# Low-weight matmuls of a merged product moved behind the high-weight ones, in the FFN of a hybrid decoder layer

## The chip, the cores and the metric

The kernel runs on one core of one Trainium2 chip. The metric is the device time of one execution in microseconds (us); lower is better. A core has TensorE (PE, with its weight loads as PEld), VectorE (DVE), ScalarE (ACT), GpSimd (POOL) and SyncE (SP), which issues most of the transfers.

## The reference

One decoder layer over a sequence of 512 with a width of 2048, all in float32. Four mixers share an input projection and an output projection, then comes a gated MLP with a causal depthwise convolution, then a last norm:

```python
D_MODEL = 2048; SEQ = 512; FFN_DIM = 5504; MIX_W = 512
...
h = rmsnorm(x, norm_mix_g[l])
proj = h @ w_in[l]
s5_u, cv_v, cv_g, lru_x, lru_g, pool_x = jnp.split(proj, split_idx, axis=-1)
...
mixed = jnp.concatenate([y_s5, y_cv, y_lru, y_pool], axis=-1)
x = x + mixed @ w_out[l]
h = rmsnorm(x, norm_ffn_g[l])
x = x + conv_gated_mlp(h, ffn_w_up[l], ffn_w_dw[l], ffn_b_dw[l], ffn_w_down[l])
...
def conv_gated_mlp(h, w_up, w_dw, b_dw, w_down):
    up = h @ w_up
    gate, val = jnp.split(up, 2, axis=-1)
    gate = causal_dwconv(gate, w_dw, b_dw)
    return (jax.nn.gelu(gate, approximate=True) * val) @ w_down
```

## The kernel before

Tensors lie with the model's width on the 128 partitions and the 512 positions of the sequence in the free dimension. Every float32 operand of a matmul is split in two fp32r parts: ScalarE casts it to a high part (`split_to`, the CAST on L106), VectorE subtracts that from the original to get the low part (the TENSOR_TENSOR on L60). A normal product (`mm3`) is three matmuls of 512 columns: high weights by high data, high weights by low data, low weights by high data.

The FFN's up and down projections are mostly done by a scheme that replaces eight block products by seven products of sums and differences of blocks, called forms (a, b, d, r1, r2, r3, r4). In those the two halves of the data, 256 columns each, lie side by side in one tile as [high | low]. The high weights of a block take one matmul of 512 columns over both halves; the low weights take one of 256 columns over the high half alone, added to columns 256 to 511 of the same bank. This is the merged product that the change touches. It stands in two functions, both called `product`:

- in `ffn_up` (L1239 to L1249), 40 output tiles by 7 forms, 280 products, each of 8 blocks `p`. Data are the tiles X0 to X7, weights `uh<form>` and `ul<form>`.
- in `seven` (L1442 to L1452), called once for each of two groups of the down projection, 8 pairs of output tiles by 7 forms, so 56 products each, of 7 blocks. Data are the tiles Y (index Y5_0 to Y5_6 in the first group), weights `dh<form>` and `dl<form>`.

Weights come as tiles of 1024 (up) or 896 columns (down) on SP's queue; for r1 and r3 a second load on GpSimd's queue adds another block in place. They are staged two products ahead; the high and low tiles have three buffers each. In `ffn_up` the finished bank is copied out whole, by `after`; in `seven` two VectorE additions of 256 columns each (`xn<-xn,pa` and `xn<-xn,pb`) add the bank's halves to the residual, which lies in the tiles xn.

Before each `seven`, `eights` does five ordinary tiles of the down projection (L1352), eight output banks at a time; the first time ScalarE copies the banks to xn (L1375). Meanwhile `forms_dn` (L1386) loads pairs of stored activations as tiles `ap` (ap5_0 to ap5_6, two buffers) on SP's queue, and makes the Y tiles from them: casts on ScalarE, and sums, multiplications and subtractions on VectorE. Its last operation, a cast and a subtraction of 4 x 256 columns, completes the forms r4, r1, r3, d and r2.

TensorE's order in these stages is the program's order. A scheduler sets the order of the other engines and of SP's queue, from a cost model of its own.

Of the kernel before, what the change touches and what calls it, by code (L numbers as in the profile page):

```python
# [15 lines left out]
P = 128  # L16
# [28 lines left out]
NP2 = 7  # L45
# [4 lines left out]
class Kernel:  # L50
# [1144 lines left out]
    def ffn_up(self, xf, rp, rstd, ub):  # L1195
        tc, nc, a = self.tc, self.nc, self.a
        IX = {"a": 0, "b": 1, "r4": 2, "r1": 3, "r2": 4, "r3": 5, "d": 6}
# [41 lines left out]
        def product(k):  # L1239
            f, form = seq[k]  # L1240
            wh, wl = staged.pop(k)
            new = form in ("a", "b", "r1")
            if new:
                bank[f, form] = self.pa() if form == "b" else self.pb() if f % 2 else self.pa()
            ps = bank[f, {"a": "a", "r2": "a", "r3": "a", "d": "a", "b": "b", "r1": "r1", "r4": "r1"}[form]]
            for p in range(8):
                x, c = xf[p][:, IX[form]], slice(p * P, p * P + P)
                self.mm(ps, wh[:, c], x.rearrange("p n c->p (n c)"), new and p == 0, False, True)
                self.mm(ps[:, 256:512], wl[:, c], x[:, 0], False, p == 7, True)  # L1249

        two = lambda t: t.rearrange("p (n c)->p n c", n=2)
        quad = lambda tag, f: ub.tile([P, 2, 2, 256], F32, tag=tag, name=f"{tag}_{f}")
# [38 lines left out]
        for k in range(len(seq)):  # L1291
            with tc.high_priority(self.hp):
                load(k + LD)
                stage(k + AH)
            product(k)
            after(k)
# [108 lines left out]
    def seven(self, g):  # L1405
        tc, nc, a = self.tc, self.nc, self.a
        W = NP2 * P
        IX = {"a": 0, "b": 1, "r4": 2, "r1": 3, "r3": 4, "d": 5, "r2": 6}
        seq = [(0, x) for x in ("a", "r1", "r2", "b", "r3")]
        for j in range(1, 9):  # L1410
            for form, back in (("a", 0), ("d", 1), ("r1", 0), ("r4", 1), ("r2", 0), ("b", 0), ("r3", 0)):
                if j - back < 8:
                    seq.append((j - back, form))
        raws, staged, bank = {}, {}, {}
        blk = lambda j, x: a["w_dns"][g, j + 8 * (x in "cd"), :, int(x in "bd")]

        def load(k):
            if k >= len(seq):
                return
            j, form = seq[k]  # L1420
            if form in ("r2", "r4"):
                return
            t = (self.wp if form == "d" else self.rp).tile([P, 1024], F32, tag="raw", name=f"d{form}{g}_{j}")[:, 0:W]
            raws[j, form] = t
            nc.sync.dma_start(t, blk(j, "c" if form in ("r1", "r3") else form))
            if form in ("r1", "r3"):
                nc.gpsimd.dma_start(t, blk(j, "d" if form == "r1" else "a"), accum_op=ADD)

        def stage(k):
            if k >= len(seq):  # L1430
                return
            j, form = seq[k]
            if form in ("r2", "r4"):
                t = raws[j, "r1"]
                self.tt(t, t, raws[j, "a" if form == "r2" else "b"], ADD)
                raws[j, form] = t
            hi = self.wq.tile([P, 1024], F32R, tag="hi", name=f"dh{form}{g}_{j}")[:, 0:W]
            lo = self.wq.tile([P, 1024], F32R, tag="lo", name=f"dl{form}{g}_{j}")[:, 0:W]
            self.split_to(hi, lo, raws[j, form])
            staged[k] = (hi, lo)  # L1440

        def product(k):  # L1442
            j, form = seq[k]
            wh, wl = staged.pop(k)
            new = form in ("a", "b", "r1")
            if new:
                bank[j, form] = self.pa() if form == "b" else self.pb() if j % 2 else self.pa()
            ps = bank[j, {"r2": "a", "r3": "a", "d": "a", "r4": "r1"}.get(form, form)]
            for p in range(NP2):
                x, c = self.xf[p][:, IX[form]], slice(p * P, p * P + P)  # L1450
                self.mm(ps, wh[:, c], x.rearrange("p n c->p (n c)"), new and p == 0, False, True)
                self.mm(ps[:, 256:512], wl[:, c], x[:, 0], False, p == NP2 - 1, True)  # L1452
            up, half, op = {"a": (0, 0, ADD), "b": (0, 0, ADD), "r2": (0, 1, ADD), "r4": (0, 1, ADD),
                            "r3": (8, 1, SUB), "r1": (8, 1, SUB), "d": (8, 0, SUB)}[form]
            x = self.x2[j + up][:, 256 * half:256 * half + 256]
            for i in range(2):
                self.tt(x, x, ps[:, 256 * i:256 * i + 256], op)

        LD, AH = 6, 2
        for k in range(LD):  # L1460
            with tc.high_priority(self.hp):
                load(k)
        yield None
        for k in range(AH):
            with tc.high_priority(self.hp):
                stage(k)
            yield None
        for k in range(len(seq)):
            with tc.high_priority(self.hp):
                load(k + LD)  # L1470
                stage(k + AH)
            product(k)
            if g == 0 and seq[k][1] == "r3" and seq[k][0] < 6:
                self.resid2(seq[k][0] + 2)
                self.resid2(seq[k][0] + 10)
            yield len(seq) - 1 - k
# [139 lines left out]
```

## Time and profile before

| | |
|---|---|
| median of 3 runs | 1885.39 us (1875.49 to 1887.56) |
| the profiled execution's own time | 1886.01 us |
| its span, first to last instruction | 1884.0 us |
| TensorE busy | 1832.3 us, 97% of the span |
| VectorE busy | 1580.4 us, 84% |
| ScalarE busy | 905.9 us, 48% |

The profile is of one execution. In the timeline, times of matmuls begin when they start and overlap with the next one; ends are modelled. "xN" at a row's end counts instructions that were merged into one row, which starts with the first of them. Brackets name what ended the idle time before a row.

### The profile page before, as it was taken

The page shows a single profiled execution, that of the slowest core. Times are in us where ns is not written, and L with a number is a line of the kernel's source. Part 1 is how long each engine was busy: PE and PEld are TensorE (multiplying, and loading weights), DVE is VectorE, ACT ScalarE, POOL GpSimd, SP SyncE. Part 2 cuts the span into 40 slices and gives each one's busy share as a digit, 9 for nine tenths or more (in the row PEclk, how much of TensorE's full clock was granted, in tenths as well). Part 3 has the DMA queues.
Part 4 walks back from the last instruction along what each step waited for, and adds up shares of the span by engine and source line. Part 5 has one row for each costly group of instructions (what it writes and reads, how often), then busy time and mean ns, then how long its engine had stood idle before and what let it go on. Part 6 is the DMA issues. An engine that isn't in the chain of part 4 may idle for free.

```text
span 1884.0 us, 25963 instructions
## 1 busy us (share of the span) xinstructions
PE 1832.3 (97%) x9610; PEld 1548.0 (82%) x9610; DVE 1580.4 (84%) x2385; ACT 905.9 (48%) x1181; POOL 209.5 (11%) x291
## 2 busy tenths in 40 slices
PE   8999999999899999999999999999999999999996
PEld 6788887888788888888888888888888788788885
DVE  8699989998695788888888888888887889878965
ACT  6322446432573555555555555555555434433443
POOL 6210020202000000000000000000001210001000
PEclk9999999999999999999999999999999999999998
DMA  6232222523345777777777777777748975577623
GB/s 207 91 97 93 94 92 93 168 84 96 106 168 169 209 192 197 201 200 203 193 203 207 193 198 199 203 207 191 200 117 269 253 202 147 165 220 188 152 83 108
DMA packets 111870, 313.56 MB, mean 166 GB/s; under 512 B 15808, under 2 KB 21952, under 8 KB 111744
## 3 DMA queue, kind: packets, MB, share of 16 engines
q1 hardware_dynamic: 91920, 249.25, 39.4%
q0 software_dynamic: 19536, 62.14, 19.6%
q8 instruction: 75, 1.23, 0.3%
q10 hardware_dynamic: 288, 0.52, 0.1%
q14 instruction: 51, 0.42, 0.1%
HBM read 289.71 MB, written 19.66 MB: 164 GB/s over the span
## 4 chain that ended last, share of the span: by engine, by line
PE 85%; DVE 7%; DMA 4%; ACT 2%; issue 1%; POOL 0%; DVEq 0%; SPq 0%; ACTq 0%; POOLq 0%
PE pa L97 55%; PE pb L97 30%; DVE lo L60 1%; DMA ap<-act 1%; DMA raw<-w_dn 1%; DMA ur<-w_up 1%; DMA raw<-w_a 1%; ACT hi L106 1%; DVE X L60 1%; DVE M L60 0%; DVE o L60 0%; DVE bk L60 0%; DVE A L63 0%; DMA av<-act 0%; DVE l_x L63 0%
## 5 line engine op out<-in xcount | busy, mean ns | idle before, releaser
L97 PE MATMUL pa<-A,hi 128*128 128x512 f32 x1312 | 413.6, 397 | 15.0 <-ACT A L73 7.3
L97 PEld LDWEIGHTS pa<-A,hi 128*128 128x128 f32 x1312 | 246.9, 190 | 74.3 <-ACT A L73 7.7
L106 ACT CAST uhr<-ur 128x1024 fp32r<-128x1024 f32 x160 | 168.0, 1050 | 228.8 <-PE pb L97 120.2
L97 PE MATMUL pa<-A,lo 128*128 128x512 f32 x656 | 258.0, 396 | 2.3 <-DVE lo L60 2.2
L60 DVE TENSOR_TENSOR ulr<-ur,uhr 128x1024 fp32r<-128x1024 f32 x160 | 195.5, 1222 | 57.2 <-ACT uhr L106 57.2
L106 ACT CAST hi<-raw 128x1024 fp32r<-128x1024 f32 (+2 forms) x128 | 132.6, 1037 | 216.3 <-PE pa L97 166.5
L97 PE MATMUL pb<-X,uhr 128*128 128x512 f32 x640 | 231.3, 401 | 1.2 <-ACT uhr L106 1.2
L97 PE MATMUL pa<-X,uhr 128*128 128x512 f32 x640 | 229.7, 399 | 0.0
L60 DVE TENSOR_TENSOR lo<-raw,hi 128x1024 fp32r<-128x1024 f32 (+2 forms) x128 | 158.4, 1239 | 47.9 <-ACT hi L106 47.4
L97 PE MATMUL pb<-X,ulr 128*128 128x256 f32 x640 | 180.6, 282 | 0.8 <-DVE ulr L60 0.8
L97 PE MATMUL pa<-X,ulr 128*128 128x256 f32 x640 | 179.7, 281 | 0.0
L1222 POOL DMA_DIRECT2D ur<-w_up x80 | 70.0, 875 | 816.3 <-DMA ur<-w_up 564.9
L97 PEld LDWEIGHTS pa<-A,lo 128*128 128x128 f32 x656 | 124.3, 190 | 31.4 <-DVE lo L60 3.1
L97 PEld LDWEIGHTS pb<-X,uhr 128*128 128x128 f32 x640 | 121.0, 189 | 31.7 <-ACT uhr L106 1.5
L97 PEld LDWEIGHTS pa<-X,uhr 128*128 128x128 f32 x640 | 120.3, 188 | 30.0
L97 PEld LDWEIGHTS pb<-X,ulr 128*128 128x128 f32 x640 | 121.6, 190 | 1.1 <-DVE ulr L60 1.1
L97 PEld LDWEIGHTS pa<-X,ulr 128*128 128x128 f32 x640 | 120.9, 189 | 0.0
L97 PE MATMUL pa<-X,uhb 128*128 128x512 f32 x320 | 114.9, 399 | 0.0
L106 ACT CAST dhr<-dr 128x896 fp32r<-128x896 f32 x64 | 60.4, 943 | 100.0 <-PE pa L97 53.1
L97 PE MATMUL pa<-X,ulb 128*128 128x256 f32 x320 | 89.9, 281 | 0.0
L63 DVE SCALAR_TENSOR_TENSOR M<-h,par,M 128x511 f32<-128x511 f32 (+29 forms) x120 | 85.1, 738 | 0.1
L60 DVE TENSOR_TENSOR xn<-xn,pa 128x256 f32<-128x256 f32 (+1 forms) x146 | 64.4, 444 | 19.6 <-PE pa L97 17.1
(346 smaller groups left out, 4217.6 us busy)
## 6 DMA issues: line engine op xcount, KB each, us to landing
ur<-w_up SPq DMA_DIRECT2D x80, 512.0 KB, 6.3
ur<-w_up POOLq DMA_DIRECT2D x80, 512.0 KB, 7.5
raw<-w_b SPq DMA_DIRECT2D x40, 512.0 KB, 3.9
ud<-w_up SPq DMA_DIRECT2D x40, 512.0 KB, 9.0
ua<-w_up SPq DMA_DIRECT2D x40, 512.0 KB, 7.2
ub<-w_up SPq DMA_DIRECT2D x40, 512.0 KB, 4.4
raw<-w_out SPq DMA_DIRECT2D x32, 512.0 KB, 3.6
dr<-w_dns SPq DMA_DIRECT2D x32, 448.0 KB, 4.0
```

Source lines behind the costliest of these rows:

```text
L60: (eng or self.nc.vector).tensor_tensor(out, x, y, op=op)
L63: self.nc.vector.scalar_tensor_tensor(out, x, s, y, op0=op0, op1=op1)
L97: self.nc.tensor.matmul(ps, lhsT=l, rhs=r, start=start, stop=stop, skip_group_check=go_on)
L106: self.nc.scalar.copy(hi, src)
L1222: nc.gpsimd.dma_start(v8(t), blk(f, "d" if form == "r1" else "a"), accum_op=ADD)
```

## The change

In both `product` functions the loop over the blocks is cut in two: first all matmuls with high weights, then all with low weights. The operands, the bank, the start flag on the first and the stop flag on the last matmul of the product stay what they were.

```diff
             for p in range(8):
                 x, c = xf[p][:, IX[form]], slice(p * P, p * P + P)
                 self.mm(ps, wh[:, c], x.rearrange("p n c->p (n c)"), new and p == 0, False, True)
-                self.mm(ps[:, 256:512], wl[:, c], x[:, 0], False, p == 7, True)
+            for p in range(8):
+                self.mm(ps[:, 256:512], wl[:, p * P:p * P + P], xf[p][:, IX[form], 0], False, p == 7, True)
...
             for p in range(NP2):
                 x, c = self.xf[p][:, IX[form]], slice(p * P, p * P + P)
                 self.mm(ps, wh[:, c], x.rearrange("p n c->p (n c)"), new and p == 0, False, True)
-                self.mm(ps[:, 256:512], wl[:, c], x[:, 0], False, p == NP2 - 1, True)
+            for p in range(NP2):
+                self.mm(ps[:, 256:512], wl[:, p * P:p * P + P], self.xf[p][:, IX[form], 0], False, p == NP2 - 1, True)
```

First place, TensorE in one product of the up projection (form r2 of output tile 5; pb574 is its bank). Before:

```order
L97 MATMUL pb574_5822<-X0_4693,uhr2_5_5872 128x512
L97 MATMUL pb574_5822<-X0_4693,ulr2_5_5873 128x256
L97 MATMUL pb574_5822<-X1_4698,uhr2_5_5872 128x512
L97 MATMUL pb574_5822<-X1_4698,ulr2_5_5873 128x256
L97 MATMUL pb574_5822<-X2_4783,uhr2_5_5872 128x512
L97 MATMUL pb574_5822<-X2_4783,ulr2_5_5873 128x256
```

And now:

```order
L97 MATMUL pb574_5822<-X0_4693,uhr2_5_5872 128x512
L97 MATMUL pb574_5822<-X1_4698,uhr2_5_5872 128x512
L97 MATMUL pb574_5822<-X2_4783,uhr2_5_5872 128x512
L97 MATMUL pb574_5822<-X3_4788,uhr2_5_5872 128x512
L97 MATMUL pb574_5822<-X4_4875,uhr2_5_5872 128x512
L97 MATMUL pb574_5822<-X5_4880,uhr2_5_5872 128x512
L97 MATMUL pb574_5822<-X6_4967,uhr2_5_5872 128x512
L97 MATMUL pb574_5822<-X7_4972,uhr2_5_5872 128x512
L97 MATMUL pb574_5822<-X0_4693,ulr2_5_5873 128x256
L97 MATMUL pb574_5822<-X1_4698,ulr2_5_5873 128x256
```

Eight matmuls of 512 columns stand in a row, then eight of 256; before, the two sizes alternated.

Second place, SP's queue ahead of the first down group, where the last activation pairs are loaded (ap5_5, ap5_6) among weights of the group (da, dr, db, dd). Before:

```order
L1391 DMA ap5_5_13183<-act15_7951 128x512
L1391 DMA ap5_5_13183<-act16_8135 128x512
L1425 DMA da0_1_13251<-w_dns 128x896
L1425 DMA dd0_1_13515<-w_dns 128x896
L1391 DMA ap5_6_13227<-act17_8319 128x512
L1391 DMA ap5_6_13227<-act18_8503 128x512
L1425 DMA dr10_1_13379<-w_dns 128x896
L1425 DMA db0_1_13444<-w_dns 128x896
```

And now:

```order
L1392 DMA ap5_5_13183<-act15_7951 128x512
L1426 DMA da0_1_13251<-w_dns 128x896
L1392 DMA ap5_5_13183<-act16_8135 128x512
L1426 DMA dd0_1_13515<-w_dns 128x896
L1426 DMA dr10_1_13379<-w_dns 128x896
L1426 DMA db0_1_13444<-w_dns 128x896
L1392 DMA ap5_6_13227<-act17_8319 128x512
L1392 DMA ap5_6_13227<-act18_8503 128x512
```

The two loads of ap5_6 moved behind dr10_1 and db0_1, and the second load of ap5_5 behind da0_1. On ScalarE the casts that read ap5_6 follow, at the place where the banks of `eights` are copied out (pb870 and on, then pa874, which is the bank that the first down product reuses). Before:

```order
L106 CAST Y5_6_13228<-ap5_6_13227 128x256
L106 CAST dhr10_0_13311<-dr10_0_13243 128x896
L106 CAST Y5_6_13228<-ap5_6_13227 128x2x256
L1375 COPY xn8_13339<-pb870_13145 128x512
L1375 COPY xn9_13341<-pb871_13146 128x512
L1375 COPY xn10_13343<-pb872_13147 128x512
L1375 COPY xn11_13345<-pb873_13148 128x512
L1375 COPY xn12_13347<-pa874_13149 128x512
```

And now:

```order
L1376 COPY xn8_13339<-pb870_13145 128x512
L1376 COPY xn9_13341<-pb871_13146 128x512
L1376 COPY xn10_13343<-pb872_13147 128x512
L1376 COPY xn11_13345<-pb873_13148 128x512
L106 CAST Y5_6_13228<-ap5_6_13227 128x256
L1376 COPY xn12_13347<-pa874_13149 128x512
```

The first cast from ap5_6 moved from ahead of the five copies to a place between the fourth and the fifth.

Third place, VectorE at the start of the first down group: the rest of the work on Y5_6, and the additions that empty bank pa878 of the group's first product into xn0. Before:

```order
L63 SCALAR_TENSOR_TENSOR ap5_6_13227<-ap5_6_13227 128x256 x2
L60 TENSOR_TENSOR dlr20_0_13359<-dr10_0_13243,dhr20_0_13358 128x896
L60 TENSOR_TENSOR dr10_0_13243<-dr10_0_13243,db0_0_13246 128x896
L60 TENSOR_TENSOR Y5_6_13228<-ap5_6_13227,Y5_6_13228 128x4x256
L60 TENSOR_TENSOR xn0_13129<-xn0_13129,pa878_13362 128x256
L60 TENSOR_TENSOR dlb0_0_13383<-db0_0_13246,dhb0_0_13382 128x896
```

And now:

```order
L60 TENSOR_TENSOR xn0_13129<-xn0_13129,pa878_13362 128x256
L63 SCALAR_TENSOR_TENSOR ap5_6_13227<-ap5_6_13227 128x256
L60 TENSOR_TENSOR dlb0_0_13383<-db0_0_13246,dhb0_0_13382 128x896
L60 TENSOR_TENSOR xn0_13129<-xn0_13129,pa878_13362 128x256
L63 SCALAR_TENSOR_TENSOR ap5_6_13227<-ap5_6_13227 128x256
L60 TENSOR_TENSOR Y5_6_13228<-ap5_6_13227,Y5_6_13228 128x4x256
```

The subtraction that completes Y5_6 moved from ahead of the two additions to behind them, and the two multiplications of ap5_6 went with it. Within the up projection the scheduler also moved one cast per output tile ahead of the activation that closes the tile's gate on ScalarE, and its subtraction on VectorE likewise.

## Rows read from the trace of the kernel before

**Rows 1.** The page: the span, and busy time by engine (TensorE's row)

```profile
span 1884.0 us, 25963 instructions
...
PE 1832.3 (97%) x9610; PEld 1548.0 (82%) x9610; DVE 1580.4 (84%) x2385; ACT 905.9 (48%) x1181; POOL 209.5 (11%) x291
```

**Rows 2.** Stretch of the up products: busy us by engine, PEclk, DMA share, GB/s

```profile
612.00:1430.00 818.00, 814.44 (x4568) 703.99 (x4566) 689.71 (x786) 434.01 (x537) 67.32 (x77) 1.00 0.73 195
```

**Rows 3.** TensorE's timeline, up products: start us, us, engine, line, op, out<-in

```profile
732.78 0.40 PE L97 MATMUL pb<-X,uhr 128*128 128x512 f32 x1
...
809.10 0.40 PE L97 MATMUL pa<-X,uhd 128*128 128x512 f32 x1
```

**Rows 4.** TensorE's timeline, starts of products in the first and second down group

```profile
1481.77 0.40 PE L97 MATMUL pb<-Y,dha 128*128 128x512 f32 x1
...
1575.76 0.40 PE L97 MATMUL pb<-Y,dhr 128*128 128x512 f32 x1
...
1672.67 0.40 PE L97 MATMUL pa<-Y,dhr 128*128 128x512 f32 x1
...
1777.02 0.39 PE L97 MATMUL pa<-Y,dhr 128*128 128x512 f32 x1
```

**Rows 5.** TensorE's timeline, mixer stage: a run of 256, a run of 512 after one

```profile
475.81 0.28 PE L97 MATMUL pb<-xl,Cpad 128*128 128x256 f32 x1
...
477.12 0.40 PE L97 MATMUL pa<-A,hi 128*128 128x512 f32 x1
...
483.58 0.40 PE L97 MATMUL pa<-lxh,hi 128*128 128x512 f32 x1
...
485.42 0.39 PE L97 MATMUL pa<-l_r,hi 128*128 128x512 f32 x1
```

**Rows 6.** TensorE's timeline: long runs in the projection, FFN standard tiles, last tiles

```profile
240.21 0.39 PE L97 MATMUL pa<-A,lo 128*128 128x512 f32 x1
...
251.34 0.40 PE L97 MATMUL pa<-A,lo 128*128 128x512 f32 x1
...
588.35 0.62 PE L97 MATMUL pa<-X,hi 128*128 128x512 f32 x2
...
607.16 0.39 PE L97 MATMUL pb<-X,lo 128*128 128x512 f32 x1
...
1849.52 0.40 PE L97 MATMUL pb<-sa,hi 128*128 128x256 f32 x2
...
1851.29 0.40 PE L97 MATMUL pa<-sa,hi 128*128 128x256 f32 x2
```

**Rows 7.** TensorE's timeline, second up product: its first high and first low matmul

```profile
614.23 0.49 PE L97 MATMUL pb<-X,uhr 128*128 128x512 f32 x1 [1.15 <-ACT uhr L106]
615.49 0.39 PE L97 MATMUL pb<-X,ulr 128*128 128x256 f32 x1 [0.77 <-DVE ulr L60]
```

**Rows 8.** Timeline, last products of the first down group: two additions, next matmul

```profile
1603.62 0.88 DVE L60 TENSOR_TENSOR xn<-xn,pb 128x256 f32<-128x256 f32 x2 [0.75 <-PE pb L97]
...
1604.64 0.47 PE L97 MATMUL pb<-Y,dhd 128*128 128x512 f32 x1 [1.06 <-ACT hi L106]
```

**Rows 9.** Timeline, transition into the first down group, all engines and SP's issues

```profile
1453.24 0.80 SPq L1391 DMA_DIRECT2D ap<-act  x2
...
1457.65 0.33 SPq L1425 DMA_DIRECT2D db<-w_dns  x1
...
1462.38 0.41 ACT L106 CAST Y<-ap 128x256 fp32r<-128x256 f32 x1 [1.26 <-DMA ap<-act]
...
1465.96 0.61 ACT L1375 COPY xn<-pa 128x512 f32<-128x512 f32 x1
...
1466.63 0.80 PE L97 MATMUL pa<-Y,dha 128*128 128x512 f32 x1 [3.51 <-ACT xn L1375]
...
1470.56 1.22 DVE L60 TENSOR_TENSOR Y<-ap,Y 128x1024 fp32r<-128x1024 f32 x1
```

**Rows 10.** DMA view, 1625 to 1665 us: issues, KB each, median us to landing

```profile
ap<-act SPq DMA_DIRECT2D x6, 256.0 KB, 3.3
```

## The prediction

> **What bounds the kernel now.** I read the page first: TensorE is busy for 1832.3 of the span's 1884.0 us [rows 1], so a saving must come out of TensorE's own time. Then the stretches by stage: in the products of the up projection (612 to 1430 us) TensorE is busy for 814.44 of 818.00 us, at a granted clock of 1.00, while VectorE has 689.71 and ScalarE 434.01 us [rows 2]. Nobody keeps it waiting there. What the change can move is the time from one matmul's start to the next one's, which I call the pitch and read from the timeline, because the durations that the trace gives for matmuls overlap.
>
> In the up products a high matmul (512 columns) and a low one (256) alternate. From 732.78 to 809.10 us lie 27 whole products, 216 pairs: 76.32 / 216 = 353.3 ns per pair, 2.827 us per product [rows 3]. The first down group runs at the same pace: 38 products of 7 pairs between 1481.77 and 1575.76, 93.99 / 266 = 353.3 ns. The second doesn't: 43 products between 1672.67 and 1777.02 take 104.35 / 301 = 346.7 ns per pair [rows 4]. Instruction for instruction the two groups are alike, so the pitch isn't a fixed price per matmul: the same sequence settles at one of several paces. That is the point on which this forecast turns.
>
> **The change, part by part.** It removes and adds no instruction: the same 3,024 pairs (280 up products of 8, 112 down products of 7) with the same weight loads stand in another order. Its price is a difference of pitches, and then what the scheduler did with the other engines.
>
> *Runs in place of pairs.* The trace of before has no up product in the new order, but it has runs of equal matmuls. A run of 256 columns between runs of 512, in the mixer stage: 11 in 477.12 - 475.81 = 1.31 us, 119.1 ns each [rows 5]. Eight of 512 right after such a run: 485.42 - 483.58 = 1.84 us, 230.0 ns each [rows 5]. Both bounds have rows as well. Best: the standard tiles of the FFN, which read the same X tiles, take 607.16 - 588.35 = 18.81 us for 83 matmuls of 512, 226.6 ns; the last tiles take 1851.29 - 1849.52 = 1.77 us for 15 of 256, 118.0 ns [rows 6]. Worst: the projection, 251.34 - 240.21 = 11.13 us for 48 of 512, 231.9 ns [rows 6]. I take the rows 5 values: they are the only ones in which a run of 512 follows a run of 256 and is short, as it will be in every product, and the 230.0 against 226.6 says that such a run starts slowly before it settles.
>
> Up product: 8 x 230.0 + 8 x 119.1 = 2.793 us against 2.827, so -0.034; 278 of the 280 (the first two are disturbed by waits) give -9.4 us. By the best rows 2.757, -0.070 each, -19.4; by the worst 2.808, -0.019 each, -5.2. Down product: 2.444 us (best 2.412, worst 2.457) against 2.473 in the slow and 2.427 in the fast group. I count 54 slow products in the first group, and 45 fast and 10 slow in the second: -1.6 + 0.8 - 0.3 = -1.1 us. Here the change spends what the lucky pace of the second group had given.
>
> *The wait for the first lo.* At the start of the up products the first low matmul waits for VectorE's ulr and starts 1.26 us after its high one (615.49 - 614.23) [rows 7]; without the wait the distance would be one pitch of 512 columns, about 0.23. Now eight high matmuls lie between: -1.0 us.
>
> *The first half of the bank.* Columns 0 to 255 of a down product are final after the high row, 7 x 119 ns = 0.83 us earlier. Where TensorE must wait for the two adds (0.88 us together, the next product starting at 1604.64 behind them [rows 8]; there is one such place per group) one of the two is out of the way: -0.44 each, -0.9 us. Elsewhere banks aren't waited for, and the earlier half is worth nothing.
>
> *What costs nothing.* The low weights are wanted 1.8 us later and the high ones are let go about 1 us earlier; both only add slack to a staging that TensorE doesn't wait for [rows 2]. Uncovered, a late lo tile would cost its subtraction, 1.2 us a time. That the casts now stand ahead of the activation on ScalarE has the same cover.
>
> *The transition into the first down group.* This part of the change isn't in the diff but in the order. The loads of the last activation pair, ap5_6, now stand behind dr10_1 and db0_1 on SP. Before, they were issued at 1453.24, and its first cast could start at 1462.38, 9.1 us later; db0_1 was issued at 1457.65 [rows 9]. With db0_1 ahead of them they go at 1458.0 or later, 4.7 us late, and land at 1467.1; if instead their buffer (ap5_4's, itself loaded later) is the last to come, I put the landing at 1469.5. ScalarE now has that cast ahead of the copy that frees product 0's bank. Before, that copy took 0.61 us from 1465.96 and product 0 began at 1466.63 [rows 9]; now it would be 1467.1 + 0.41 + 0.61 + 0.1 = 1468.2, or 1470.6: +1.6 to +3.9, middle +2.8. Then VectorE: the subtraction that completes Y5_6 stood at 1470.56 to 1471.78 [rows 9], ahead of product 0's two adds; now it is behind both, so it ends about 3.4 us after product 0 (an add of 0.44 as in rows 8, a multiply put at the same, the subtraction's 1.22 [rows 9], a cast put at the same, gaps). Product 1 wants it at its seventh high matmul, 6 x 0.23 us after its start (up to twice that at a lower granted clock): +0.7 to +2.1, middle +1.4. The second group has the same move, but the same kind of load landed there in 3.3 us [rows 10], so most of the delay should be absorbed: 0 to +3, I take +0.5. Together +4.7, say +5, from +2.3 to +9.
>
> **Sum.** -9.4 - 1.1 - 1.0 - 0.9 + 5 = -7.4 us. The profiled execution took 1886.0 us (span 1884.0 and 2.0 around it), 0.6 above the median of the three runs, so I forecast 1878.6, that is **1879 us**.
>
> **A rule that speaks against the change.** The measured pitches depend on the neighbours: 353.3 and 346.7 ns for one and the same pair [rows 3, 4], 344.6 from the separate runs [rows 6]. The Trainium skill, "TensorE: Matmul & The Clock Gate", section "Back-to-back issue gap", gives the isolated gap at full clock as N/2.4 + 2.5 ns, a price that knows no neighbours; by it a pair would be about 325 ns in either order, an estimate from that page, and regrouping would gain nothing. The trace is above it in every pair, and differs between identical sequences. What such a rule makes of the result is the second rival.
>
> **The rivals.** (1) *The runs lock at the best pitch.* If every product reaches 226.6 and 118.0 ns at once: -19.4 up; -0.061 x 54, -0.015 x 45 and -0.061 x 10 down, -4.6; -1.9 for the two waits, +5: 1865.1 us. For it speaks that rows 6 has the same X tiles; against it, the slow start of rows 5, and that 8 matmuls are few. (2) *Order doesn't matter:* a pair costs what it costs. Then only -1.9 + 5 remain: 1889 us. Against it, rows 3 to 6; for it, that no row shows this order on an up product. (3) *The down transition eats the gain*, the case that ends slower: ap5_6, loaded last, holds both the bank's copy and Y5_6. It decides from the point where it costs over 6.8 us, if the pitch gives only the worst rows (-5.2 up, +0.3 down, -1.9); with the pitch that I take, from 12.4 us. If the loads miss one whole landing more (9.1 us) on top of +3.9, it costs 13: 1892 us with the worst pitch. For it: the landing of 9.1 us and two queues that both moved the wrong way. Against it: before, TensorE already waited 3.51 us there for that copy [rows 9], and part of the delay hides in work that goes on. That the change doesn't do what it says is excluded: TensorE's order is fixed by the program there, and shows eight and eight.
>
> **How the numbers follow.** Forecast 0.58, with a range of its own from 1873 (transition +2.3, pitch between forecast and best) to 1886 (worst pitch, transition +6); rival 1 0.15, rival 2 0.12, rival 3 0.15. Below 1864 I leave some 0.08 (rival 1 with a cheap transition), above 1890 some 0.11 (most of rival 3, a little of rival 2): 1864 to 1890. A measurement of this kernel tells about 1% from no change, 18.9 us here. Under 1866.5 lies about three quarters of rival 1 and next to nothing of the forecast: 0.12. Over 1904 would need a transition of more than 25 us: 0.04. The rest, 0.84, is within 1%.
>
> **What would show it.** In the profile after: 27 up products in about 75.4 us instead of 76.32 (74.4: rival 1; 76.3: rival 2), with 512s that begin at 230 to 240 ns and fall to 227 inside a product; the first low matmul of the second up product no longer 1.26 us behind; product 0 of the first down group starting 2 to 4 us later after the end of its eight tiles than before (3.5 us), with a gap inside product 1; two adds that no longer stand in a row. The prediction is wrong if the settled pace of a product lies outside 2.757 to 2.827 us, or if a wait on a cast or subtraction turns up within the up products.

## The result and the profile after

| | before | after |
|---|---|---|
| median of 20 runs each | 1874.57 us (1868.18 to 1887.59) | 1884.89 us (1878.39 to 1891.42) |
| the profiled execution | 1886.01 us | 1878.93 us |
| up products, 27 of them in the profile | 76.32 us | 75.42 us |
| ratio after to before | | 1.0050, 95% interval 1.0031 to 1.0068 |

The changed kernel is slower by 0.5%; the forecast was 0.3% faster. Yet between the two profiled executions the time went from 1886.0 to 1878.9 us, 7.1 us less, close to the sum that the prediction had worked out (7.4). Both are true at once, and the experiments had to find out how. The ratio is the recorded one, not the quotient of the two medians (1.0055), here and below.

The page of the changed kernel, its span and the row of busy times [rows 1]:

```profile
span 1877.0 us, 26005 instructions
...
PE 1819.4 (97%) x9610; PEld 1549.6 (83%) x9610; DVE 1565.2 (83%) x2385; ACT 906.1 (48%) x1181; POOL 207.6 (11%) x291
```

TensorE is busy for 12.9 us less. TensorE's timeline of the changed kernel, up products (columns as in [rows 3]; x8 is a run of eight):

```profile
733.77 2.00 PE L97 MATMUL pb<-X,uhr 128*128 128x512 f32 x8
735.61 1.12 PE L97 MATMUL pb<-X,ulr 128*128 128x256 f32 x8
736.57 2.00 PE L97 MATMUL pa<-X,uhb 128*128 128x512 f32 x8
...
809.19 0.40 PE L97 MATMUL pa<-X,uhr 128*128 128x512 f32 x1
...
1476.40 0.40 PE L97 MATMUL pa<-Y,dhd 128*128 128x512 f32 x1
...
1510.65 0.40 PE L97 MATMUL pa<-Y,dhd 128*128 128x512 f32 x1
```

From 733.77 to 809.19 us lie 27 products: 2.793 us each, where [rows 3] gave 2.827. The high row takes 735.61 - 733.77 = 1.84 us, 230 ns a matmul, the low row 0.96 us, 120 ns. In the first down group 14 products lie between 1476.40 and 1510.65: 2.446 us each, against 2.473 there before [rows 4].

The start of the up products, second product, same view [rows 7]:

```profile
613.39 2.11 PE L97 MATMUL pb<-X,uhr 128*128 128x512 f32 x8 [1.08 <-ACT uhr L106]
615.34 1.11 PE L97 MATMUL pb<-X,ulr 128*128 128x256 f32 x8
616.34 2.12 PE L97 MATMUL pb<-X,uhr 128*128 128x512 f32 x8
```

The wait for the first low weights is gone. The product takes 616.34 - 613.39 = 2.95 us; in the profile of before it took 5.48. That is more than the wait itself: in that execution the granted clock stood at 0.61 behind it (columns as in [rows 2]):

```profile
615.00:619.00 4.00, 3.51 (x12) 3.04 (x13) 3.90 (x5) 2.12 (x3) 0.00 (x0) 0.61 1.03 311
```

The transition into the first down group, all engines and SP's issues [rows 9]:

```profile
1449.98 0.81 SPq L1392 DMA_DIRECT2D ap<-act  x2
...
1453.18 0.44 ACT L106 CAST Y<-ap 128x256 fp32r<-128x256 f32 x1
1453.48 1.59 ACT L1376 COPY xn<-pa 128x512 f32<-128x512 f32 x3
...
1454.15 3.26 PE L97 MATMUL pa<-Y,dha 128*128 128x512 f32 x7 [4.66 <-ACT xn L1376]
...
1458.08 1.09 DVE L60 TENSOR_TENSOR dr<-dr,db 128x896 f32<-128x896 f32 x1
1458.26 1.54 PE L97 MATMUL pa<-Y,dhr 128*128 128x512 f32 x6
...
1459.74 1.09 DVE L60 TENSOR_TENSOR dlb<-db,dhb 128x896 fp32r<-128x896 f32 x1
1460.75 0.42 DVE L60 TENSOR_TENSOR xn<-xn,pa 128x256 f32<-128x256 f32 x1
...
1461.08 0.42 DVE L63 SCALAR_TENSOR_TENSOR ap<-ap 128x256 f32<-128x256 f32 x1
1461.53 1.04 ACT L106 CAST Y<-ap 128x1024 fp32r<-128x1024 f32 x1 [3.09 <-DVE ap L63]
...
1462.61 1.23 DVE L60 TENSOR_TENSOR Y<-ap,Y 128x1024 fp32r<-128x1024 f32 x1 [1.11 <-ACT Y L106]
...
1463.89 0.50 PE L97 MATMUL pa<-Y,dhr 128*128 128x512 f32 x1 [4.09 <-DVE Y L60]
...
1465.49 2.67 PE L97 MATMUL pa<-Y,dhr 128*128 128x512 f32 x6
```

Read it from its end upwards. TensorE stops for 4.09 us ahead of the seventh high matmul of product 1, for the subtraction that completes Y5_6. That waits for ScalarE's cast, the cast for VectorE's last multiplication of ap5_6 (1461.08), and this stands in VectorE's order behind the second addition of product 0 (1460.75). In the stretches of TensorE behind the wait (columns as in [rows 2]) the granted clock is 0.57 and comes back by 1468:

```profile
1464.00:1468.00 4.00, 4.00 (x14) 3.43 (x15) 1.85 (x3) 0.94 (x1) 0.00 (x0) 0.57 1.10 266
1468.00:1472.00 4.00, 4.00 (x26) 3.56 (x25) 2.05 (x4) 1.88 (x2) 0.87 (x1) 1.00 1.07 261
```

Against the profile of before that is no extra loss: there too the granted clock was low at this place, 0.72, 0.50 and 0.92 in the three stretches of 4 us from 1464 us on, although product 1 did not wait. The run with the old transition, below, has 0.57 from 1456 to 1460 us and 1.00 from there on.

The end of the first down group, VectorE and TensorE [rows 8]:

```profile
1594.36 0.42 DVE L60 TENSOR_TENSOR xn<-xn,pb 128x256 f32<-128x256 f32 x1 [0.69 <-PE pb L97]
1594.69 1.22 DVE L60 TENSOR_TENSOR lo<-raw,hi 128x1024 fp32r<-128x1024 f32 x1
1595.83 0.42 DVE L60 TENSOR_TENSOR xn<-xn,pb 128x256 f32<-128x256 f32 x1
...
1596.39 2.24 PE L97 MATMUL pb<-Y,dhd 128*128 128x512 f32 x7 [2.07 <-DVE xn L60]
...
1605.85 0.70 PE L97 MATMUL pb<-sa,hi 128*128 128x512 f32 x2 [0.71 <-DVE xn L60]
```

The first half of the bank is added early, as foreseen. But now VectorE has the 1.22 us of the next tile's subtraction between the two additions, and TensorE waits 2.07 us where it had waited 1.06 [rows 8].

### The profile page after: what moved, and what is told of

It reads as the page before. It is cut to its first block, busy times and chain, and to the rows that moved or that the text cites. A ratio compares the mean times of both kernels' runs of the same rounds, so it can differ in the third digit from the quotient of the medians.

```text
span 1877.0 us, 26005 instructions
## 1 busy us (share of the span) xinstructions
PE 1819.4 (97%) x9610; PEld 1549.6 (83%) x9610; DVE 1565.2 (83%) x2385; ACT 906.1 (48%) x1181; POOL 207.6 (11%) x291
## 4 chain that ended last, share of the span: by engine, by line
PE 85%; DVE 8%; DMA 4%; ACT 2%; issue 1%; SPq 0%; POOL 0%; DVEq 0%; ACTq 0%; POOLq 0%
PE pa L97 55%; PE pb L97 30%; DVE lo L60 1%; DMA ap<-act 1%; DMA ur<-w_up 1%; DMA raw<-w_dn 1%; DVE X L60 1%; ACT hi L106 1%; DVE M L60 0%; DVE o L60 0%; DVE bk L60 0%; DVE Y L60 0%; DVE xn L60 0%; DMA par<-par 0%; DVE l_x L63 0%
## 5 line engine op out<-in xcount | busy, mean ns | idle before, releaser
L97 PE MATMUL pa<-A,lo 128*128 128x512 f32 x656 | 257.7, 396 | 3.9 <-DVE lo L60 3.9
L97 PE MATMUL pb<-X,uhr 128*128 128x512 f32 x640 | 160.5, 393 | 1.1 <-ACT uhr L106 1.1
L97 PE MATMUL pa<-X,uhr 128*128 128x512 f32 x640 | 160.3, 392 | 0.0
L97 PEld LDWEIGHTS pb<-X,uhr 128*128 128x128 f32 x640 | 115.1, 189 | 22.0 <-ACT uhr L106 1.3
L97 PEld LDWEIGHTS pa<-X,uhr 128*128 128x128 f32 x640 | 115.1, 189 | 20.6
L97 PEld LDWEIGHTS pb<-X,ulr 128*128 128x128 f32 x640 | 87.3, 190 | 6.2
L97 PEld LDWEIGHTS pa<-X,ulr 128*128 128x128 f32 x640 | 87.3, 190 | 6.2
L97 PE MATMUL pa<-X,ulr 128*128 128x256 f32 x640 | 89.2, 282 | 0.0
L97 PE MATMUL pb<-X,ulr 128*128 128x256 f32 x640 | 89.2, 282 | 0.0
L97 PE MATMUL pa<-X,uhb 128*128 128x512 f32 x320 | 80.1, 392 | 0.0
L60 DVE TENSOR_TENSOR ulb<-ub,uhb 128x1024 fp32r<-128x1024 f32 x40 | 49.0, 1225 | 34.4 <-ACT uhb L106 34.4
```

Source lines behind the costliest of these rows:

```text
L60: (eng or self.nc.vector).tensor_tensor(out, x, y, op=op)
L97: self.nc.tensor.matmul(ps, lhsT=l, rhs=r, start=start, stop=stop, skip_group_check=go_on)
```

## The experiments

The two theories at the start. A: alternating pairs have two paces, 346.7 and 353.3 ns; most executions of before run their up products at the fast one, and the profiled one had the slow one. B: the pace of the up products is the same in every execution, and the loss lies in the waits of the down groups. In the table "groups" gives the usual time of a product in each of the two down groups, and times in brackets are the least and the largest.

### The kernel before, twice more

> The kernel before, unchanged, in one more profiled execution. Theory A (two paces): the pairs of a 512 and a 256 settle at 346.7 or 353.3 ns, and which one is open per execution; most executions have the fast pace through the up products. An execution near 1870 to 1877 us shows up products of about 2.774 us (346.7 x 8) over most of 610 to 1400 us, one near 1885 us shows 2.827 us (353.3 x 8). Theory B (one pace in the up products): 2.827 us there in every execution, and what separates an execution of 1872 us from one of 1886 us are waits and stretches at the lower granted clock outside them.

> The same kernel a second time, same expectations: theory A gives 2.774 or 2.827 us per up product, the time following the pace by about 15 us (0.053 x 278); theory B gives 2.827 us both times whatever the time is.

They took 1873.12 and 1871.14 us. TensorE's timeline of the first of the two, 27 up products from start to start:

```profile
734.71 0.39 PE L97 MATMUL pa<-X,uhr 128*128 128x512 f32 x1
...
809.59 0.39 PE L97 MATMUL pb<-X,uhr 128*128 128x512 f32 x1
```

74.88 / 27 = 2.773 us, 346.7 ns a pair, and so through the whole stage, in both. The stage lasts 780.9 and 782.4 us, and 797.2 in the profile that the prediction read. The down groups draw for themselves: 2.427 and 2.473 us in the first execution, 2.473 and 2.427 in the second. Theory A; B is out, since the pace does differ. From the times alone: of the 112 executions of before that were timed in the five comparisons with intervals, 66 lie below 1879 us (the lower group, median 1871.2) and 46 above (the upper group, median 1886.9), 15.7 us apart; the pace of the up products accounts for 0.054 x 278 = 15.0.

### One part of the change alone

The up products alone (the first hunk of the diff), and the down products alone (the second).

> Runs of eight in the up products only; the down groups alternate as before. On SP and ScalarE the last activation pair still stands late at the transition, as in the changed kernel, so this run has the pitch of up and the transition and lacks the down pitch. Theory A: up products 2.793 us in the profile, against 2.774 in a usual execution of before, +5.3 us, and a few us for the transition: +5 to +9 us on the median of before. Theory B: -9.4 us from the up pitch and a transition that costs more than that; the profile would show it in waits of 15 us or more around the down groups.

> Runs of seven in the down products only; the up products alternate as before, and the loads of the last activation pair keep their old place ahead of the weights. Theory A: down products 2.446 us against 2.427 at the fast pace, 110 of them, +2.1 us at most, less where a group would have run at the slow pace (2.473, -1.5 a group); no transition cost; the up products are free to take either pace, so the runs should spread as widely as those of before: 0 to +3 us. Theory B (the transition and the down groups make the loss): with the transition's order undone, at most 1 us from before; if it lies in the runs of seven themselves, +10 us.

| | median | before, same comparison | ratio | up product | groups |
|---|---|---|---|---|---|
| up alone | 1880.5 (1878.0 to 1885.5) | 1872.5 | 1.0026 (1.0001 to 1.0051) | 2.793 | 2.427, 2.427 |
| down alone | 1875.3 (1869.9 to 1890.7) | 1872.5 | 1.0016 (0.9982 to 1.0051) | 2.773 | 2.447, 2.447 |

Both came as theory A had them. With the up products alternating, 7 of 12 executions lie at 1870 to 1876 and 5 at 1887 to 1891, as in before; with runs of eight the upper group is gone and so is the lower. The up edit also carries the new order of the transition: the three stretches from the last up product to the end of the second five tiles take 268.4 us with it, 261.4 and 263.4 in the two executions above, and 258.2 with the down edit alone, whose queue has the old order. One profile of each does not tell what the runs of seven do there. Over all profiles of this document these stretches take 257.7 to 263.9 us in the eleven with the old order, with runs of seven or alternating, and 266.5 to 268.4 us in the three with the new one. So it is the new order that puts some 6 us in, by the means of the two sets (267.6 against 261.4).

### The transition taken back

```diff
-            for p in range(8):
+            n = 8 if k < 275 else 1
+            rows = [(lo, q + r) for q in range(0, 8, n) for lo in (0, 1) for r in range(n)]
+            for i, (lo, p) in enumerate(rows):
...
```

The rest is the changed kernel. That the last five up products alternate is enough for the scheduler to put SP's queue back.

> The changed kernel, but the last five of the 280 up products alternate as before. With that, SP's queue is the same as in the kernel before: the last activation pair is loaded ahead of dr10_1 and db0_1 again. Theory A: the transition was worth 7 to 8 us of the changed kernel's loss (its three stretches from the end of the up products to the end of the second five tiles took 266.5 us, against 258.2 with the down runs and the old order): 1877 us, 7 us below the changed kernel and 0 to +5 on before. Rival (the runs cost, not the transition): no more than 2 us below the changed kernel, +8 to +10 on before.

> The changed kernel once more, as the partner of the run with five alternating products: +8 to +12 us on before; up products at 2.793 us and down products at 2.446 us in the profile, whatever its time; a wait inside product 1 of the first down group again, and the last wait of that group at 2.1 us where before has 1.1.

The changed kernel took 1883.6 us (1881.1 to 1887.5, ratio 1.0045, 1.0019 to 1.0071), the one with the old transition 1877.4 (1873.8 to 1881.6, ratio 0.9996, 0.9966 to 1.0025): 6.2 us of the loss lie in that order. What is left, 6.9 us above the lower group of before in this comparison (1870.5), stays with the runs. The before of this comparison has 15 of its 29 executions in the upper group and a median of 1882.4, so the +8 to +12 and 0 to +5 us that were expected on before came only against its lower group (+13.1 and +6.9); against that median they are +1.2 and -5.0. The up products of both stand at 2.793 us. TensorE's timeline with the transition taken back, products 0 and 1 and the start of product 2:

```profile
1456.46 3.32 PE L97 MATMUL pa<-Y,dha 128*128 128x512 f32 x7 [3.72 <-ACT xn L1379]
...
1460.44 1.78 PE L97 MATMUL pa<-Y,dhr 128*128 128x512 f32 x7
1462.06 0.98 PE L97 MATMUL pa<-Y,dlr 128*128 128x256 f32 x7
1463.33 1.89 PE L97 MATMUL pa<-Y,dhr 128*128 128x512 f32 x7 [0.28 <-DVE xn L60]
```

The seven high matmuls of product 1 stand in a row again, without the 4.09 us and the slow stretch after it. The three stretches take 262.1 us against 267.8 in the changed kernel of this comparison. That is still 3.9 us above the down edit alone, whose order is the same: single profiles of one order differ by as much. The rival, that the runs cost and not the order, is out.

### Runs of other lengths

```diff
-            for p in range(8):
+            n = (1, 2, 1, 4, 1, 8, 1, 16)[k // 35]
+            rows = [(lo, q + r) for q in range(0, 8, min(n, 8)) for lo in (0, 1) for r in range(min(n, 8))]
+            if n == 16 and form in ("d", "r4", "r3"):
+                rows = rows[8:] + rows[:8]
+            for i, (lo, p) in enumerate(rows):
...
```

> The 280 up products in eight stretches of 35, whose products take their matmuls in runs of 1, 2, 1, 4, 1, 8, 1 and 16 (1: alternating as before; 16: run of eight, and every second product or so turned round with its low row first, so that equal runs of neighbours join). The down groups are as before. Theory A1 (the interval belongs to the place in a run: 233, 236, 228, 233, 231, 226, 227, 227 ns in a run of 512s and 113, 119, 120, ... in a run of 256s, as the changed kernel shows): 8 x (233 + 113) = 2.768 us a product in runs of 1, (233 + 236 + 113 + 119) x 4 = 2.804 in runs of 2, (930 + 472) x 2 = 2.804 in runs of 4, 2.793 in runs of 8, 2.781 on average in runs of 16. Rival A2 (each change of size has a fixed price, 18 ns, from 2.793 against 8 x 226.6 + 8 x 118 = 2.757): 3.045, 2.901, 2.829, 2.793, 2.777. Of the two paces: if a stall at the start of the stage draws the pace once, the four alternating stretches may still differ, since other runs lie between; if what stands ahead sets the pace, the three that follow a stretch of longer runs all show the same one, 2.773 or 2.827.

TensorE's timeline, for each of the first four stretches (runs of 1, 2, 1, 4) the starts of two products that lie 20 apart:

```profile
641.63 0.39 PE L97 MATMUL pa<-X,uhb 128*128 128x512 f32 x1
...
697.09 0.39 PE L97 MATMUL pb<-X,uhr 128*128 128x512 f32 x1
...
738.83 0.40 PE L97 MATMUL pa<-X,uhb 128*128 128x512 f32 x1
...
794.57 0.40 PE L97 MATMUL pa<-X,uhr 128*128 128x512 f32 x1
...
836.77 0.40 PE L97 MATMUL pa<-X,uhb 128*128 128x512 f32 x1
...
893.30 0.40 PE L97 MATMUL pb<-X,uhr 128*128 128x512 f32 x1
...
935.50 0.40 PE L97 MATMUL pa<-X,uhb 128*128 128x512 f32 x1
...
991.63 0.40 PE L97 MATMUL pa<-X,uhr 128*128 128x512 f32 x1
```

The time was 1879.16 us, in one execution. 55.46 / 20 = 2.773 us in runs of 1, 2.787 in runs of 2, then 2.827 for the same alternation, 2.807 in runs of 4. Further on it is 2.827, 2.793 (runs of 8), 2.827 and 2.785 (runs of 16, 2.781 expected). A fixed price per change of size (A2) is out: it wanted 3.045 and 2.901 for runs of 1 and 2. A1 is near, with 2 and 4 off by up to 0.02. The stretch at the start had drawn the fast pace; each of the three that follow longer runs has the slow one. So within one execution the same matmuls take 2.773 or 2.827 us, by what stands ahead of them. The starts, one by one, show what the paces are, in ns from start to start (512, 256, 512, ...; the fast ones from the two executions of before with the fast pace, the slow one from the profile of before):

```
fast:  230 117 230 116 ...     or  231 113 232 118 231 112 233 117 ...
slow:  241 120 236 113 233 117 241 120 236 113 233 117 ...
```

The slow pace is a cycle of three pairs (1060 ns), the fast one of one or two.

### Neighbours' equal rows put together

```diff
+            rows = [(lo, p) for lo in ((1, 0) if form in ("d", "r4", "r3") else (0, 1)) for p in range(8)]
...
```

> Every up product in two runs of eight as in the changed kernel, but the forms d, r4 and r3 take their low row first, so that rows of equal size of neighbouring products stand together (8 changes of size in 7 products where the changed kernel has 14). The down groups alternate as before, and the loads of the last activation pair keep their old place. Theory A: 2.781 us per up product on average in every execution (2.793 where no runs join, 2.757 if the settled pitch came at once), 2.2 us more than before at its fast pace over the stage, about 2 us less in waits there, and one pace only: the runs lie within some 8 us, without the group 15 us above the others, and the median within 3 us of that of before. Theory B (the transition makes the whole loss and the pitch none): 4 us or more faster than before.

Median 1873.4 us (1868.5 to 1877.4), ratio 0.9964 (0.9935 to 0.9994) to a before that stood at 1882.4 in this comparison, 15 of its 29 executions in the upper group. The product takes 2.785 us on average, where 2.781 was expected; no execution is in the upper group, and the median is 2.9 us above the 14 in the lower (1870.5). "Within 3 us" holds against that lower group alone. Against the whole of this before it is 9 us faster, which by itself would read like theory B; the pace and the missing upper group decide for A. Its queue has the old transition, so this says what runs joined in this way are worth by themselves: they sit between the two paces of alternation.

### What sets the pace

Every 14th product in one of 20 other patterns (H high, L low, S a high one cut into 256 + 256 columns), alternating between:

```diff
+            kick = "HL" * 8
+            if k >= 8 and (k - 8) % 14 == 0:
+                kick = KICKS[(k - 8) // 14]
...
```

> The 280 up products alternate as before, but every 14th (form r4) takes its 16 matmuls in another order, or with one or more high matmuls cut in two pieces of columns, 20 patterns in all: turned round (low first), runs of 2, 3, 4, 8 in front, a 512 cut into 256 + 256, 128 + 384 or 384 + 128, a 256 cut into 128 + 128. Between two patterns lie 13 alternating products, whose pitch shows the pace that the pattern leaves. Theory K1 (the pace is set by the last few matmuls' sizes alone): each pattern leaves one pace of its own, and some of the 20 leave 2.773 us, so that alternation could be held there. K2 (only a wait or a rise of the clock can lead into the fast pace, and any break of the alternation leads to the slow one, as runs of 2, 4 and 8 did): 2.773 or 2.827 up to the first pattern, 2.827 after each of them. K3 (a short break leaves the pace as it was): one pace all through, except behind the long runs.

One execution, 1875.18 us. K2 and K3 fall: patterns led from slow to fast, from fast to slow, or kept the pace. TensorE's timeline around pattern 17 (HHL HLHL... LL), nine products ahead of it and nine behind:

```profile
1238.92 0.40 PE L99 MATMUL pb<-X,uha 128*128 128x512 f32 x1
...
1264.37 0.40 PE L99 MATMUL pa<-X,uhr 128*128 128x512 f32 x1
...
1275.52 0.40 PE L99 MATMUL pa<-X,uhr 128*128 128x512 f32 x1
...
1300.48 0.40 PE L99 MATMUL pb<-X,uhd 128*128 128x512 f32 x1
```

25.45 / 9 = 2.828 us ahead, 24.96 / 9 = 2.773 behind. K1, one pace for each pattern, holds only in part: what a pattern does also hangs on the point of the cycle at which it comes.

That shows best in the two kernels with the cut S, once in each stage (the fifth product) and in every 14th product. The latter's edit in the up products:

```diff
-                self.mm(ps, wh[:, c], x.rearrange("p n c->p (n c)"), new and p == 0, False, True)
+                y, w = x.rearrange("p n c->p (n c)"), 256 if p == 0 and k % 14 == 8 else 512
+                for u in range(0, 512, w):
+                    self.mm(ps[:, u:u + w], wh[:, c], y[:, u:u + w], new and p == 0, False, True)
...
```

> The order of before, but in one up product (the fifth) and in one product of each down group (the fifth) the first high matmul of 512 columns is cut into two of 256. Behind such a cut the run with the 20 patterns showed the fast pace where the slow one had stood. If the cut leads to the fast pace from either one: up products at 2.773 us in every execution, down products at 2.427 us, and 1869 us (871 us of up and down products at the fast pace; the executions of before near 1871 us have it in up and by chance in the groups), no execution of the upper group near 1885 us. If it leads from fast to slow as well as from slow to fast, or only by chance: two groups 15 us apart again, with other shares. If the pace were no cause of the two groups of times: as before, median and shares.

> The same cut in every 14th product, 20 in the up products and 4 in each down group, so the profile shows what a cut does from either pace. Each costs some 15 to 30 ns in its product (2.802 us was seen in place of 2.773), under 1 us in all. If the cut leads to the fast pace from either one: 1869 to 1870 us, no upper group. If it turns fast into slow and slow into fast: stretches of 14 products that alternate between 2.773 and 2.827 us and a time between the two groups, 1877 us, in every execution.

(The 871 us in a parenthesis of the first is a slip; nothing hangs on it.) Both expectations of a faster kernel failed. With one cut: 1872.7 us (1868.7 to 1891.0), 8 executions low and 4 high, ratio 0.9992 (0.9956 to 1.0028). With a cut in every 14th product all 12 executions are high: 1886.8 us (1883.2 to 1889.2), ratio 1.0064 (1.0039 to 1.0089). TensorE's timeline of the latter, ahead of the first cut and later on:

```profile
623.65 0.39 PE L97 MATMUL pa<-X,uhb 128*128 128x512 f32 x1
...
637.52 0.28 PE L97 MATMUL pb<-X,uhr 128*128 128x256 f32 x1
...
897.61 0.40 PE L97 MATMUL pb<-X,uhr 128*128 128x512 f32 x1
...
973.94 0.40 PE L97 MATMUL pa<-X,uhr 128*128 128x512 f32 x1
```

Five products of 2.774 us, then the cut at 637.52, and from there on 2.827 (27 products in 76.33 us). The starts say why: where the cut met the fast pace, with no wait beside it, it led to the slow one each time, five times in the profiles of the two kernels, and each time in the cycle of one pair (230 117). From the slow one it led to the fast one only where a 236 and then a 232 were the last two high matmuls ahead of it (once in each down group of this kernel, and in the run of 20 patterns). In the up products the cuts soon come at one and the same other point of the cycle of three, which keeps it slow. What a single cut does to the other fast cycle (231 113 232 118 ...) is in no profile. The one-cut kernel's profile is one of its high executions; its 8 low ones have no profile, and they are more than this rule would lead one to expect, since most executions of before run at the fast pace. So the rule is shown for these points of the cycle and no others.

### The pace held

So one needs a known point first. Runs of eight give one: behind them the profiles have 230 to 234, 117 to 119, then 240 or 241, and where the alternation goes on from there, the slow cycle. Here the cycle is broken where the 241 stands. No instruction is added:

```diff
+            rows = "HL" * 8
+            if k % 140 == 3:
+                rows = "H" * 8 + "L" * 8
+            elif k % 140 == 4:
+                rows = "HLHHLL" + "HL" * 5
...
```

and the same with 7, at the fourth and fifth product, in each down group.

> The order of before, with no instruction added, but two products changed in the up projection near its start (and again half-way), and two in each down group: the fourth takes runs of eight (seven), which leaves the slow cycle at a known point (234, 117, 241, 120, 236, 113 ns) whatever stood ahead, and the fifth takes high low, high high low low, high low ..., which breaks that cycle where a 241 comes next. In the run with the 20 patterns high high low low at that point led from slow to fast. Theory: the pace is fixed by the sequence and by the point of the cycle at which it is broken. Then up products settle at 2.773 us in every execution, from the sixth product on, and again behind the second break (runs of eight from the fast pace: 0.04 us for the two products), both down groups at 2.427 us, and all executions lie between 1867 and 1874 us, median 1870, without the group near 1885. If the break leads to the slow pace here, all lie near 1885 us, as with the cut in every 14th product. If chance decides, both groups appear.

Median 1871.0 us (1866.7 to 1873.4), all 12 executions in the lower group, ratio 0.9948 (0.9917 to 0.9979) to a before that stood at 1885.6 in this comparison, 11 of its 17 executions in the upper group. If chance decided, with the share of 66 in 112, twelve low ones in a row would come about once in 570 times, an estimate. The second break, half-way through the up products, interval by interval in ns:

```
run of eight:   231 224 231 235 230 231 232 227 | 112 119 120 120 120 120 120 121
HL HH LL HL...: 233 117 241 238 116 118 233 117 231 113 233 117 231 112 233 118
next product:   230 113 232 118 231 112 232 119 230 112 233 118 231 111 234 117
```

After it TensorE's timeline has 27 products between these two starts, 74.88 / 27 = 2.773 us:

```profile
734.58 0.39 PE L97 MATMUL pb<-X,uhr 128*128 128x512 f32 x1
...
809.46 0.39 PE L97 MATMUL pa<-X,uhr 128*128 128x512 f32 x1
```

Both down groups stand at 2.427 for some 40 products. Behind a product with a short wait near the end (2.63 us) both go on at 2.473, so the pace holds only up to the next wait. This version does not run faster than the lower group of before (1871.2), it has no upper one: its mean is 7.0 us below that of the 112 executions of before (1877.5). Its slowest execution (1873.4) is below the fastest of the changed kernel (1878.4).

## Why the prediction was wrong

**The pitch of the runs: right.** 2.793 us an up product was forecast and measured, in four profiles; 2.447 a down product against 2.444. Neither the best pitch (first rival) nor the indifferent order (second rival, with the rule of the Trainium skill, "TensorE: Matmul & The Clock Gate", section "Back-to-back issue gap") came. By the isolated gap given there a matmul's price hangs on its columns alone; here one and the same pair took 346.7 or 353.3 ns inside one execution. One reading behind the forecast was off, without harm: the run of 512 at 483.58 [rows 5] isn't short but goes on for over 20 matmuls, and 230.0 ns is the pitch of its first eight.

**The baseline: the step that failed.** The prediction says: "The profiled execution took 1886.0 us (span 1884.0 and 2.0 around it), 0.6 above the median of the three runs, so I forecast 1878.6." It took the 353.3 ns of one execution for the price of the kernel. It had seen that the same sequence "settles at one of several paces", and applied that within the execution, group by group, but not from one execution to the next. The three times shown, 1875.49, 1885.39 and 1887.56, already held both groups. Against the fast pace the up products lose 0.020 x 278 = 5.6 us where the sum has a gain of 9.4: 15.0 us of difference from this step alone. A rival with that price was wanted, and none of the three is it. Nor did the prediction's own sign of being wrong catch it: 2.793 us lies inside 2.757 to 2.827. That the profile came out 7.1 us faster, so near the sum, is partly luck: its execution is the second fastest of the twenty, the up products gave 12.6 us where 10.4 were forecast (9.4 and the 1.0 of the wait), and the down projection cost 5.9 where 3.0 were.

**The wait for the first low weights: right, and too small.** -1.0 was forecast. Against the same profile the second product gave back 2.5 us (5.48 to 2.95), since there the granted clock was low behind the wait; against another execution of before (3.91), which had the same wait (0.75 us in place of 0.77) and kept a granted clock of 1.00, it was 1.0.

**The two additions: wrong in sign.** -0.44 a group was forecast. The halves did separate, and VectorE's order put a subtraction of 1.22 us between them: the wait went from 1.06 to 2.07 us. What was not foreseen is that the next stretch got some of it back. TensorE's wait for a bank of the five tiles that follow fell to 0.71 us, from 3.17 in the timeline of before:

```profile
1614.99 0.70 PE L97 MATMUL pb<-sa,hi 128*128 128x512 f32 x2 [3.17 <-DVE xn L60]
```

It is 0.44 with the down edit alone and 0.89 in the second profile of the changed kernel, but 2.63 with the transition taken back, so how much comes back differs from one profile to the next.

**The transition: right in sum, not in its parts.** +5, from 2.3 to 9, was forecast; taking it back gave 6.2 us by the medians and 5.7 by the stretches. Product 0 waited 4.66 us for its bank in place of 3.51, +1.15 where +2.8 was forecast; other profiles have 3.91 and 5.98 with the new order, and 2.51 to 3.95 with the old. Product 1 waited 4.09 where +1.4 was forecast (4.16 in the second profile, 2.88 with the up edit alone, nothing with the old order). The chain through VectorE was the one named, but Y5_6 was complete 5.6 us after the end of product 0 and not 3.4: two operations on other weight tiles, 1.09 us each, stand ahead of the first addition and between the two (1458.08 and 1459.74), and ScalarE's cast, put at 0.44, took 1.04.

**What stays open.** Against the lower group of before, the median of the changed kernel is 13.7 us up. Two profiles of each (1878.9 and 1884.4; 1873.1 and 1871.1) are 9.6 us apart, and show +3.0 in the up products, +4.8 in the three stretches of the transition, +1.4 in the second group. The other 4 us are no stage of the kernel: these profiles lie 3.2 us below the median of the changed kernel, and about 1 above that of the lower group. What makes executions of one kernel at one pace differ by some 10 us (1878 to 1891 for the changed kernel) is not placed. What draws the pace at a wait isn't shown either: behind one, the profiles have either pace, and between waits it never changed by itself.

## What to carry to other kernels

A profile is one draw. Before its time is used as a baseline, hold it against each single time and not only the median: where the times fall into two groups, look for a stage that settles at two paces, and take the forecast against each. Where the trace shows that a fixed sequence on TensorE has more than one pace, put a run of known length and a break at a known place at its start, and the kernel keeps the good one up to a wait; the down groups here lost it behind one near their end. And when a reordering frees a result early, read in the engine's order what the scheduler will put into the gap.

## What was not expected of the hardware

A sequence of alternating matmuls of 512 and 256 columns, at a granted clock of 1.00 and with nothing to wait for, repeats one of two cycles, 346.7 or 353.3 ns a pair (1.9%), over more than 270 products without changing; stretches of products in runs of 2, 4 and 8 left the slow one behind them, and a break at the right point of the slow cycle left the fast one. After a wait of 4.09 us the granted clock of TensorE stood at 0.57 for 4 us. After one and the same wait at the start of the up products (0.75 to 0.77 us) it stood at 0.61 for 4 us in one execution and at 1.00 in another.
